# A hybrid decoder step on one core: gate logits from bfloat16 thirds over 99 contraction rows, with every engine's order found anew

## The chip, the core and the metric

One Trainium2 chip, one of its cores. A core has a matrix engine (TensorE, PE in the profile), a vector engine (VectorE, DVE), a scalar engine (ScalarE, ACT), a general engine (GpSimd, POOL) and an engine that here only issues DMAs (SyncE, SP). Each runs its own list of instructions in order; semaphores tie the lists together. PE's loads of weights (the stationary operand) are shown as PEld. The metric is the device time of one execution in microseconds; the kernel before was timed three times: 1186.76, 1187.25 and 1187.62 us, median 1187.25.

## The reference, cut to what matters

The reference is one layer of a decoder with two mixers side by side, for a prompt of 2048 tokens and for 8 samples of 8 tokens: dilated window attention, and gated linear attention (GLA) with 4 heads, key width 64 and value width 128. The change touches the gate of the second alone. The combined input projection gives, among others, 16 low-rank gate columns `g_lr` per token; from them come 4 x 64 gate logits:

```python
z = h @ w_in
q, k, v, qb, kb, vb, g_lr, gate_a, gate_b = jnp.split(z, split_points(), axis=-1)
log_a = jax.nn.log_sigmoid((g_lr @ w_gate_up + b_gate).astype(jnp.float32)) / GATE_TAU
o_b, s_fin = gla_chunked(heads(qb, H_B) * (DK_B ** -0.5), heads(kb, H_B), heads(vb, H_B),
                         heads(log_a, H_B), s0)
```

`g_lr` has 16 columns (GATE_RANK), `w_gate_up` is 16 x 256, `b_gate` has 256 entries, and everything is float32. The logs of the forget gates are summed over tokens, so the decay between any two tokens of a chunk hangs on them.

## The kernel before, in words

The program runs in stages that are woven together. The prompt is 16 tiles of 128 tokens. First come the projections for the window attention and that attention itself (matmuls `s`, transposes `t`, matmuls `O` at L1099 to L1132); then the projections `g`, `vb` and `gb` (matmuls at L1834, accumulators `acc_g`, `acc_vb`, `acc_gb`); last the output projection (`Y`, L2192) with the attention of the samples over their caches (`OS`, L2449). Large projections are split into two float16 parts and take three products. Dot products of cached keys (`pr` on POOL, L1689) fill the middle.

GLA runs beside `g`, `vb` and `gb`: one unit for the samples ("smp", 64 tokens), then eight units e0 to e7 of 256 prompt tokens (two chunks of 128). For each, `gla_core` (L838) loads the keys and queries (`zqk`) and the 16 gate columns (`zg`, L845) from device memory, where the projection has put them (L1452). It transposes `zqk` on PE (`ptg`, L870), and `zg` too: `pg` (L878), one PE transpose per 128 tokens in float32. ACT copies `pg` to `gT` (L879), a tile of 17 rows whose last row holds ones (a memset on POOL fills the tile first, L866). Two float32 matmuls with `wgu` (16 rows of `w_gate_up`, one row of `b_gate`) give the logits `u` for 256 tokens (L882). From there ACT and DVE make the log-sigmoid `la` (L888 to L891) and the decay `d` (L893). Then come seven levels: at each, PE makes scores `sc` and `sd` (L931), DVE selects them into `Ac` (L948), and `decay()` lets POOL scale keys (L907) and DVE scale queries (L911) and multiply the decays (L917) for the next level. After the levels PE makes the state update `U` (L1991) and the outputs `O` (L1999, L2005).

What runs beside it on POOL are `gw` (L1461), `Ac` (L855) and `prod` (L848); SP issues every DMA of the kernel, in one queue.

The order of all this is written out: after the program is traced, `in_order` (L747) chains each engine's instructions in the order of a long table of numbers, `ORDER`, one list for each of PE, DVE, ACT, POOL and SP. Where an instruction waits for a semaphore, all that stands behind it in its engine's list waits too.

## Time and profile before

| what | before |
|---|---|
| median of three runs | 1187.25 us (1186.76 to 1187.62) |
| profiled execution | 1188.94 us, of which the span from the first to the last instruction is 1187.2 |
| PE busy | 1158.4 us (98% of the span) |
| DVE / ACT / POOL busy | 909.4 / 739.2 / 547.0 us (77%, 62%, 46%) |
| chain that ended last | 89% PE, 7% DVE, 2% ACT |
| granted clock of PE | 0.998 of full, mean |

A row of the view of groups or of one line reads: line, engine, operation, output<-inputs, shapes, then busy time or durations. In a source view "374/374/478" is the least, median and greatest length in ns. A timeline row gives the start in us, the length in us, the engine and the operation; "x4" merges four records, and "[0.65 <-PE sd_e L931]" is the idle time ahead of it and who ended it. A row of waits gives who waited for whom: total us, times, longest. A row of windows gives, for a stretch of time, the busy time of PE, PEld, DVE, ACT and POOL with the number of instructions, then the clock, the share of DMA engines and GB/s. Matmuls are pipelined: their records overlap, so what one costs PE in a dense run is the time from its start to the next start.

### The profile page before, as it was taken

To read this page: it belongs to the slowest core of one execution; us is meant where nothing else is said; L and a number is where in the kernel's file an instruction comes from. 1 tells how busy PE (TensorE), PEld (TensorE's weight loads), DVE (VectorE), ACT (ScalarE), POOL (GpSimd) and SP (SyncE) were. 2 spreads that over 40 slices of the span, in tenths; PEclk is the share of its full clock that TensorE was granted. 3 is DMA by queue.
4 is the path that set the end of the run, shared out by engine and by line. 5 is a ranking of instruction groups with operands and counts; after the bars stand their busy time and mean duration, and the time that the engine had idled before them with its cause. 6 is when DMAs were issued, how large, how long until landed. Compare 5 with 4: busy or idle time off the path is not lost.

```text
span 1187.2 us, 28796 instructions
## 1 busy us (share of the span) xinstructions
PE 1158.4 (98%) x10386; PEld 713.4 (60%) x10386; DVE 909.4 (77%) x2540; ACT 739.2 (62%) x2042; POOL 547.0 (46%) x475
## 2 busy tenths in 40 slices
PE   5999999999999899999999999999999999999998
PEld 2544575566666666766777766646656656555543
DVE  7988788898888968778786755688988989734551
ACT  6655798788779967878777642654676654421220
POOL 0156444566548445662444567664545454311210
PEclk9999999999999999999999999999999999999999
DMA  8568967778976898899999878766773487999962
GB/s 295 192 196 215 254 170 167 187 230 256 216 199 179 205 250 286 271 255 277 273 267 269 249 255 233 220 195 200 253 241 114 139 283 253 332 400 403 379 201 80
DMA packets 235840, 283.24 MB, mean 239 GB/s; under 512 B 116193, under 2 KB 146866, under 8 KB 232626
## 3 DMA queue, kind: packets, MB, share of 16 engines
q1 hardware_dynamic: 235698, 281.40, 78.3%
q8 instruction: 82, 1.34, 0.5%
q14 instruction: 60, 0.49, 0.1%
HBM read 183.02 MB, written 75.24 MB: 218 GB/s over the span
## 4 chain that ended last, share of the span: by engine, by line
PE 89%; DVE 7%; ACT 2%; issue 1%; DMA 1%; POOL 0%; SPq 0%; DVEq 0%; POOLq 0%; ACTq 0%
PE Y L2192 12%; PE acc_g L1834 7%; PE acc_vb L1834 7%; PE acc_qkb L1834 7%; PE acc_k L1834 7%; PE acc_v L1834 7%; PE acc_q L1834 7%; PE acc_gb L1834 7%; PE t L1117 5%; PE s L1099 5%; PE O L1132 4%; PE OS L2449 2%; PE sc_e L931 2%; PE tm L2157 1%; PE O L2005 1%
## 5 line engine op out<-in xcount | busy, mean ns | idle before, releaser
L1689 POOL TENSOR_TENSOR pr<-k,qb 128x512 f32<-128x512 f32 x128 | 170.6, 1333 | 104.6 <-DVE sck L1690 86.2
L1834 PEld LDWEIGHTS <-hr 128*128 128x128 f16 x1824 | 165.1, 98 | 84.9 <-issue 3.5
L1132 PE MATMUL O<-v,pt 128*128 128x64 f16 x1800 | 211.6, 193 | 3.0 <-POOL pt L1084 1.9
L1110 ACT ACTIVATE p<-p,st 128x256 f32<-128x256 f32 (+1 forms) x384 | 173.3, 453 | 32.5 <-DVE st L1107 31.4
L2192 PE MATMUL Y<-w_o,mh 128*128 128x512 f16 x768 | 188.9, 379 | 0.1
L1132 PEld LDWEIGHTS <-pt 128*128 128x128 f16 x1800 | 146.0, 100 | 59.0 <-issue 3.7
L1834 PEld LDWEIGHTS <-hl 128*128 128x128 f16 x1248 | 117.4, 99 | 95.4 <-issue 3.3
L1084 POOL TENSOR_TENSOR pt<-p,pt 128x512 f16<-128x512 f32 (+1 forms) x80 | 95.2, 1190 | 164.9 <-ACT pt L1081 76.3
L1117 PE MATMUL t<-ident,p 128*128 128x128 f32 x600 | 149.6, 287 | 0.3 <-ACT p L1110 0.2
L1834 PE MATMUL acc_g<-w_g,hr 128*128 128x256 f16 (+1 forms) x768 | 131.6, 277 | 0.1
L1099 PE MATMUL s<-kk,qq 128*128 128x256 f16 (+1 forms) x512 | 115.3, 265 | 2.2 <-DVE st L1107 2.2
L1834 PE MATMUL acc_v<-w_v,hl 128*128 128x512 f16 x384 | 115.3, 385 | 1.1 <-ACT hl L1207 1.1
L1834 PE MATMUL acc_vb<-w_vb,hr 128*128 128x512 f16 x384 | 114.8, 379 | 0.0
L2192 PEld LDWEIGHTS <-mh 128*128 128x128 f16 x768 | 70.8, 98 | 68.0 <-issue 3.6
L1834 PE MATMUL acc_k<-w_k,hl 128*128 128x512 f16 x384 | 110.8, 379 | 0.0
L1834 PE MATMUL acc_q<-w_q,hl 128*128 128x512 f16 x384 | 110.5, 379 | 0.0
L1107 DVE CUSTOM_DVE_ANT_0 p<-s,m3w,scl_s 128x128 f32<-128x128 f32 (+1 forms) x256 | 92.8, 395 | 21.6 <-PE s L1099 12.5
L1690 DVE TENSOR_REDUCE sck<-pr 128x8 f32<-128x512 f32 x128 | 87.4, 682 | 24.7 <-POOL pr L1689 23.9
L1834 PE MATMUL acc_gb<-w_gb,hr 128*128 128x512 f16 x384 | 97.6, 380 | 0.0
L1117 PEld LDWEIGHTS t<-ident,p 128*128 128x128 f32 x600 | 80.9, 141 | 23.4 <-ACT p L1110 2.9
L1834 PE MATMUL acc_qkb<-w_qkb,hr 128*128 128x512 f16 x288 | 84.7, 379 | 0.0
L1110 ACT ACTIVATION_READ_ACCUMULATOR p<-p,st 128x1 f32 x384 | 73.2, 191 | 0.0
(545 smaller groups left out, 2461.4 us busy)
## 6 DMA issues: line engine op xcount, KB each, us to landing
k<-in_cache_k_win SPq DMA_DIRECT2D x104, 256.0 KB
sv_b<-in_cache_v_win SPq DMA_DIRECT2D x24, 1024.0 KB
hr<-h_d SPq DMA_DIRECT2D x44, 512.0 KB
qb<-q_d SPq DMA_DIRECT2D x64, 256.0 KB
oc<-o_d SPq DMA_DIRECT2D x48, 264.0 KB
o_d<-o SPq DMA_DIRECT2D x64, 132.0 KB
x<-in_x_prompt SPq DMA_DIRECT2D x16, 512.0 KB
h_d<-hl SPq DMA_DIRECT2D x16, 512.0 KB
```

Of the source, the lines that this page charges most:

```text
L931: PE.matmul(sc[j][k0 : k0 + 64, o : o + wide], k[js, t0 : t0 + 64], qv[js, t0 // (2 * B) : t0 // (2 * B) + max(1, 32 // B), 1, :], start=T ...
L1084: POOL.tensor_tensor(l, f, h, ALU.subtract)
L1099: PE.matmul(s_ps[:, i * w : (i + 1) * w], q, k, start=(n == 0), stop=(n == len(prods) - 1),)
L1107: DVE.tensor_tensor_reduce(s[:, sl], s_ps[:, sl], mask, neg, BIG, ALU.add, ALU.min, nmf(i))
L1110: ACT.activation(s[:, sl], s[:, sl], AF.Exp, bias=nmf(i), scale=-1.0, accum_out=denf(i))
L1117: PE.transpose(p_ps[:, i * P : (i + 1) * P], t["s"][:, i * P : (i + 1) * P], ident[:])
L1132: PE.matmul(o_, t["pt"][:, c, (i * nb + b) * P : (i * nb + b + 1) * P], vf(i, b)[:, d : d + HD], start=(b + n == 0), stop=(b == nb - 1 and ...
L1689: POOL.tensor_tensor(pr[:], kt, qt, ALU.mult)
L1690: DVE.tensor_reduce(out, pr[:].rearrange("p (u k d) -> p u k d", u=2, k=4), AX.X, ALU.add)
L1834: PE.matmul(z, a_[:, k, :], w[:, p_, k, cols], start=(k == 0 and i == 0), stop=(k == KT - 1 and i == 2),)
L2192: PE.matmul(Y[:], a_[:, k, :], w_[:, part, k, :512], start=(i == 0), stop=(i == len(prods) - 1),)
L2449: PE.matmul(OS[32 * x : 32 * x + 32, 0:256], ps(x), vs_[bb][:, 256 * u : 256 * u + 256], start=(i == 0), stop=(i == 13),)
```

## The change

Each gate column is written as a sum of three bfloat16 numbers (first, second, third), and so is each weight and bias. Six of the nine products of parts are kept (third x first, first x first, second x first, first x second, second x second, first x third), and instead of six matmuls the parts lie side by side along the contraction: 6 x 16 rows of features, and three rows of ones against the three parts of the bias, 99 rows. PE contracts them all in one bfloat16 matmul per 128 outputs.

- On POOL, per unit: a copy that narrows `zg` into three places of `gz` (`spread`, first parts), a subtraction for the rest `res`, a copy of `res` into two places (second parts), and a subtraction that writes the third parts. `gz` is one tile for all units, filled with ones once. The memset of `gT` is gone.
- On PE: `pg` transposes 99 bfloat16 columns of `gz` against a bfloat16 identity instead of 16 float32 columns of `zg`; `u` is a bfloat16 matmul.
- On ACT the copy `pg` to `gT` has 99 rows and stays bfloat16.
- Once, at the start of the stage: `wgf` is loaded (two DMAs, as `wgu` was), split into three parts by two ACT casts and two DVE subtractions, and six DMAs lay the parts out in `wgu` (99 x 256); a memset and a cast on POOL make `gz` and `identb`.
- The table `ORDER` is new for every engine.

Lines behind L862 stand 16 lines later in the changed file, those behind L1960 29 lines later: L931 is L947 there, L1999 is L2028.

```diff
--- before.py
+++ after.py
@@ -51,695 +51,695 @@
 ORDER = {
     "PE": (
-        "0 10 6 1-5 11 7 18 8 12 19-20 13 21 14 22 9 74 15 23 16 75 24 17 90 25 91 76 92 77 "
...
+        "0-7 10 18-19 11 20 12 21-22 13-16 74 23 17 8 24 9 25 75 90 76 91-99 77 100-103 78 "
...
@@ -835,6 +835,8 @@
         DVE.scalar_tensor_tensor(out, a[:n], 1.5, r[:n], ALU.add, ALU.mult)
 
 
+    GK = 99
+
     def gla_core(pools, st, row0, n, C, levels, mask, tagp, full=None):
 
         gl, gt, ps_t, ps_s, ps_p = pools
@@ -862,8 +864,22 @@
 
         kq = gt.tile([P, 2, 2, n], F32, name=f"kq_{tagp}", tag="kqg", bufs=3)
         kT, qT = kq[:, 0], kq[:, 1]
-        gT = gt.tile([17, n], F32, name=f"gT_{tagp}", tag="gT", bufs=2)
-        POOL.memset(gT[:], 1.0)
+        gz = st["gz"]
+        res = gt.tile([P, nch, 16], F32, name=f"res_{tagp}", tag="res")
+
+        def spread(first, count, x):
+            POOL.tensor_copy(
+                gz[:C, :nch, first : first + 33 * count].rearrange(
+                    "p c (s f) -> p c s f", f=33
+                )[:, :, :, :16],
+                x.unsqueeze(2).to_broadcast([C, nch, count, 16]),
+            )
+
+        spread(16, 3, zg[:C])
+        POOL.tensor_tensor(res[:C], zg[:C], gz[:C, :nch, 16:32], ALU.subtract)
+        spread(32, 2, res[:C])
+        POOL.tensor_tensor(gz[:C, :nch, 0:16], res[:C], gz[:C, :nch, 32:48], ALU.subtract)
+        gT = gt.tile([GK, n], BF16, name=f"gT_{tagp}", tag="gT", bufs=2)
         for c in range(nch):
             pt = ps_p.tile([P, 512], F32, name=f"ptg_{tagp}_{c}", tag="PT")
             for i in range(4):
@@ -873,14 +889,14 @@
             pv = pt[:, : 4 * C].rearrange("p (a c) -> p a c", a=4)
             ACT.activation(qT[:, :, c * C : (c + 1) * C], pv[:, 0:2, :], AF.Copy, scale=0.125)
             ACT.activation(kT[:, :, c * C : (c + 1) * C], pv[:, 2:4, :], AF.Copy)
-        pg = ps_p.tile([P, 512], F32, name=f"pg_{tagp}", tag="PT")
+        pg = ps_p.tile([P, 1024], BF16, name=f"pg_{tagp}", tag="PT")
         for c in range(nch):
-            PE.transpose(pg[:16, c * C : (c + 1) * C], zg[:C, c, :], ident[:C, :C])
-        ACT.activation(gT[:16, :], pg[:16, :n], AF.Copy)
+            PE.transpose(pg[:GK, c * C : (c + 1) * C], gz[:C, c, :GK], st["identb"][:C, :C])
+        ACT.activation(gT[:], pg[:GK, :n], AF.Copy)
         u = ps_p.tile([P, 512], F32, name=f"u_{tagp}", tag="PT")
         for p in range(2):
             PE.matmul(
-                u[:, p * n : (p + 1) * n], st["wgu"][:, p * P : (p + 1) * P], gT[:, :],
+                u[:, p * n : (p + 1) * n], st["wgu"][:, p * P : (p + 1) * P], gT[:],
                 start=True, stop=True,
             )
         la = gt.tile([P, 2, n], F32, name=f"la_{tagp}", tag="gt", bufs=2)
@@ -1948,16 +1964,29 @@
             SP.dma_start(
                 masks[r0 : r0 + 64], A["c_gmask"][r0 : r0 + 64, :, r0 // 2 : r0 // 2 + 32]
             )
-        wgu = gst.tile([17, 256], F32, name="wgu")
-        SP.dma_start(wgu[:16, :], A["w_gate_up"][0])
-        SP.dma_start(wgu[16:17, :], A["b_gate"])
+        wgf = gst.tile([17, 2, 256], F32, name="wgf")
+        SP.dma_start(wgf[:16, 0, :], A["w_gate_up"][0])
+        SP.dma_start(wgf[16:17, 0, :], A["b_gate"])
+        wgp = gst.tile([17, 3, 256], BF16, name="wgp")
+        ACT.activation(wgp[:, 0], wgf[:, 0], AF.Copy)
+        DVE.tensor_tensor(wgf[:, 1], wgf[:, 0], wgp[:, 0], ALU.subtract)
+        ACT.activation(wgp[:, 1], wgf[:, 1], AF.Copy)
+        DVE.tensor_tensor(wgp[:, 2], wgf[:, 1], wgp[:, 1], ALU.subtract)
+        wgu = gst.tile([GK, 256], BF16, name="wgu")
+        for part, r0, m in ((0, 0, 16), (0, 16, 16), (0, 32, 17), (1, 49, 16), (1, 65, 17),
+                            (2, 82, 17)):
+            SP.dma_start(wgu[r0 : r0 + m, :], wgp[:m, part])
+        gz = gst.tile([P, 2, GK + 17], BF16, name="gz")
+        POOL.memset(gz[:], 1.0)
+        identb = gst.tile([P, P], BF16, name="identb")
+        POOL.tensor_copy(identb[:], ident[:])
         Sbd = []
         ident64 = gst.tile([P, 64], F32, name="ident64")
         for r0 in (0, 64):
             DVE.tensor_scalar(
                 ident64[r0 : r0 + 64], ident[r0 : r0 + 64, r0 : r0 + 64], 0.125, None, ALU.mult
             )
-        st = {"wgu": wgu, "ident64": ident64}
+        st = {"wgu": wgu, "ident64": ident64, "gz": gz, "identb": identb}
         for i in range(2):
             t = gst.tile([P, 2, 256], F32, name=f"Sbd{i}")
             POOL.memset(t[:], 0.0)
```

The new lists differ from the old ones by short moves nearly everywhere; half of PE's matmuls stand at most 4 places from where they stood. Three places follow. The names carry the unit (e5, e6), the level of the scores and a buffer number at the end.

PE at the gate logits of unit e6 (`pg` and `u`), while the levels of e5 run; before:

```order
L878 MATMUL pg_e6_14484<-ident_79,zg_e6_14459 16x128
L1834 LDWEIGHTS hr_15_14366
L1834 MATMUL acc_gb_15_14612<-w_gb_12118,hr_15_14366 128x512
L878 MATMUL pg_e6_14484<-ident_79,zg_e6_14459 16x128
L2005 MATMUL O_8_13354<-vb_8_13347,full_10188 128x128
L1834 LDWEIGHTS hr_15_14366
L1834 MATMUL acc_gb_15_14612<-w_gb_12118,hr_15_14366 128x512
L1999 MATMUL O_8_13354<-Sbd0_10184,kq_e4_12900 128x256
L882 MATMUL u_e6_14488<-gT_e6_14468,wgu_10178 128x256 x2
L931 MATMUL sc_e5_16_13831<-kq_e5_13482 64x32 x2
```

and with the change:

```order
L1850 LDWEIGHTS hr_15_14410
L1850 MATMUL acc_gb_15_14660<-w_gb_12150,hr_15_14410 128x512
L2028 MATMUL O_8_13394<-Sbd0_10200,kq_e4_12936 128x256
L894 LDWEIGHTS gz_10193
L894 MATMUL pg_e6_14532<-identb_10195,gz_10193 99x128
L894 LDWEIGHTS gz_10193
L894 MATMUL pg_e6_14532<-identb_10195,gz_10193 99x128
L2034 MATMUL O_8_13394<-vb_8_13387,full_10204 128x128 x2
L2028 MATMUL O_8_13394<-Sbd0_10200,kq_e4_12936 128x256
L2034 MATMUL O_8_13394<-vb_8_13387,full_10204 128x128
L898 LDWEIGHTS wgu_10186
L898 MATMUL u_e6_14536<-gT_e6_14517,wgu_10186 128x256
```

`pg` now stands directly behind the first inter-chunk `O` and ahead of the other products; four `O` products and no `acc_gb` stand between it and `u`, and weight loads have rows of their own, since float32 matmuls load theirs within the instruction.

POOL at the same time, with the scaling of e5's keys (`kq_e5`, one row per level) and `gw`; before:

```order
L907 TENSOR_TENSOR kq_e4_12900<-kq_e4_12900,sums_e4_12932 128x4x64
L907 TENSOR_TENSOR kq_e5_13482<-kq_e5_13482,d_e5_13511 128x256
L907 TENSOR_TENSOR kq_e5_13482<-kq_e5_13482,sums_e5_13514 128x128x2
L907 TENSOR_TENSOR kq_e5_13482<-kq_e5_13482,sums_e5_13514 128x64x4
L1461 TENSOR_TENSOR gw_13_14518<-so_gb13_14511,gnw_395 128x512
L907 TENSOR_TENSOR kq_e5_13482<-kq_e5_13482,sums_e5_13514 128x32x8
```

and with the change:

```order
L923 TENSOR_TENSOR kq_e5_13522<-kq_e5_13522,d_e5_13555 128x256
L923 TENSOR_TENSOR kq_e5_13522<-kq_e5_13522,sums_e5_13558 128x128x2
L923 TENSOR_TENSOR kq_e5_13522<-kq_e5_13522,sums_e5_13558 128x64x4
L1477 TENSOR_TENSOR gw_13_14566<-so_gb13_14559,gnw_395 128x512
L881 TENSOR_TENSOR gz_10193<-res_e6_14512,gz_10193 128x2x16
L923 TENSOR_TENSOR kq_e5_13522<-kq_e5_13522,sums_e5_13558 128x32x8
L857 TENSOR_TENSOR Ac_e6_14509<-ident64_10197,dd_e6_14507 128x512
L871 CAST gz_10193<-zg_e7_15257 128x2x3x16
L879 TENSOR_TENSOR res_e7_15266<-zg_e7_15257,gz_10193 128x32
```

The last of e6's four operations (`gz<-res_e6,gz`) now stands between `gw_13` and the scaling for level 8, where nothing stood; e7's first copy follows two places later.

SP's queue where the sample's gate columns are loaded; before:

```order
L1952 DMA wgu_10178<-in_w_gate_up 16x256
L1701 DMA k3_6_2_7964<-in_cache_k_win 128x512
L1257 DMA hr_12_12136<-h_d_72 128x2048
L1457 DMA ga_d_65<-so_g19_12282 128x256
L1257 DMA hr_13_12363<-h_d_72 128x2048
L1953 DMA wgu_10178<-in_b_gate 1x256
L1699 DMA qb_6_2_7962<-q_d_58 128x512
L845 DMA zg_smp_10248<-zg_d_62 64x16
L843 DMA zqk_smp_10246<-zqk_d_61 64x512
L1704 DMA k2_6_3_8170<-in_cache_k_win 128x512
L1452 DMA zg_d_62<-zgs_9_12172 128x16
```

and, a little further down the queue with the change:

```order
L1715 DMA qb_6_6_8070<-q_d_58 128x512
L1717 DMA k3_6_6_8072<-in_cache_k_win 128x512
L847 DMA zg_e0_10619<-zg_d_62 128x2x16
L1470 DMA ga_d_65<-so_g010_12452 128x256
L845 DMA zqk_e0_10617<-zqk_d_61 128x2x512
L1468 DMA zg_d_62<-zgs_10_12449 128x16
L1978 DMA wgu_10186<-wgp_10181 16x256
L1978 DMA wgu_10186<-wgp_10181 17x256 x2
L1978 DMA wgu_10186<-wgp_10181 16x256
L1978 DMA wgu_10186<-wgp_10181 17x256
L1978 DMA wgu_10186<-wgp_10181 16x256
L1717 DMA k3_6_3_8168<-in_cache_k_win 128x512
```

The six copies into `wgu` stand ahead of the next load of cached keys, behind the loads of the first units; before, `wgu` was loaded from the inputs ahead of them.

1360 rows, old and new, of the table ORDER are left out of this document.

## The prediction

> **What bounds the kernel now.** I read the page first: engine shares, then the chain that ended last.
>
> ```profile
> span 1187.2 us, 28796 instructions
> PE 1158.4 (98%) x10386; PEld 713.4 (60%) x10386; DVE 909.4 (77%) x2540; ACT 739.2 (62%) x2042; POOL 547.0 (46%) x475
> PE 89%; DVE 7%; ACT 2%; issue 1%; DMA 1%; POOL 0%; SPq 0%; DVEq 0%; POOLq 0%; ACTq 0%
> ```
>
> PE covers 98% of the span and is 89% of the chain. Since a busy PE may still be a waiting PE (records overlap), I looked next at what PE waited for.
>
> ```profile
> PE mx_v L1269 <- DVE w_v L1326: 13.5, 1, 13.5
> PE s L1099 <- DVE st L1107: 2.2, 6, 0.6
> PE O L1132 <- POOL pt L1084: 1.9, 4, 0.6
> PE sc_e L931 <- DVE kq_e L911: 1.5, 1, 1.5
> ```
>
> All of PE's idle time is 1187.2 - 1158.4 = 28.8 us, and 13.5 us of it is one wait at the very start, which nothing here touches. So 15.3 us are left in the whole rest: PE is the bound, and PE time that goes away should come off the end nearly one for one. The changed lines run only between 700 and 950 us (the gated-linear-attention stage), so the chain of that stretch, cut into three windows (690 to 780, 780 to 870, 870 to 960 us), matters most:
>
> ```profile
> by line: PE acc_vb L1834 36.4%; PE acc_g L1834 35.7%; PE O_s L2058 4.1%; PE U_s L2091 3.8%; PE u_e L882 3.5%; PE ptg_e L870 3.4%; DVE kq_e L911 2.3%; PE acc_gb_s L1518 1.9%; PE acc_gb_s L1521 1.1%; PE sc_smp L931 1.1%; PE pg_e L878 0.9%; is
> by line: PE acc_gb L1834 53.3%; PE sc_e L931 12.8%; PE O L2005 6.4%; PE O L1999 5.2%; PE sd_e L931 4.3%; PE U L1991 3.7%; DVE kq_e L911 3.2%; PE u_e L882 3.0%; PE ptg_e L870 2.6%; PE U_s L2091 1.5%; PE ptk_e L973 1.1%; PE pg_e L878 0.8%; DV
> by line: PE acc_gb L1834 34.2%; PE sc_e L931 8.1%; PE O L1999 3.8%; DVE kq_e L911 3.5%; PE U L1991 3.2%; issue 3.1%; DVE Sbd L2012 3.0%; PE O L2005 3.0%; DVE Ac_e L948 2.6%; PE sd_e L931 2.2%; ACT mh L2158 2.0%; PE u_e L882 1.9%; DVE w_o L1
> ```
>
> The matmul that makes the gate logits, u (L882), is 3.5%, 3.0% and 1.9% of three 90 us windows: 3.2 + 2.7 + 1.7 = 7.6 us stand on the path that sets the end. Its transposes pg (L878) stand there too, with 0.9% and 0.8% in the first two.
>
> **The change, part by part.** Matmuls are pipelined, so I price them from start to the next start, not by their own length.
>
> ```profile
> 703.37 0.65 PE L882 MATMUL u_smp<-gT_smp,wgu 17*128 17x64 f32 x4
> 703.95 0.39 PE L1834 MATMUL acc_vb<-w_vb,hr 128*128 128x512 f16 x1
> ...
> 716.33 0.27 PE L878 MATMUL pg_e<-ident,zg_e 128*16 128x128 f32 x1
> 716.44 1.42 PE L1834 MATMUL acc_g<-w_g,hr 128*128 128x272 f16 x11
> 717.70 0.27 PE L870 MATMUL ptg_e<-ident,zqk_e 128*128 128x128 f32 x1
> ...
> 736.27 1.13 PE L882 MATMUL u_e<-gT_e,wgu 17*128 17x256 f32 x4
> 737.33 0.82 PE L1834 MATMUL acc_vb<-w_vb,hr 128*128 128x512 f16 x3
> ...
> 945.97 0.22 PE L2157 MATMUL tm<-ident,mt 128*128 128x128 f16 x1
> ...
> 947.76 0.67 PE L2157 MATMUL tm<-ident,mt 128*128 128x128 f16 x9
> ...
> L882 PE MATMUL u_e<-gT_e,wgu x32: 374/374/478, 736.3 to 945.4; 17*128 17x256 f32 x32
> L878 PE MATMUL pg_e<-ident,zg_e x16: 272/273/278, 716.3 to 943.5; 128*16 128x128 f32 x16
> ```
>
> *Removed: float32 u.* The program asks for two matmuls per chunk of 256 tokens, the trace holds 32 records for 8 chunks: each float32 matmul goes through PE twice. One chunk's four records take 737.33 - 736.27 = 1.06 us of PE. Eight chunks: 8.5 us; the sample's: 703.95 - 703.37 = 0.58 us.
>
> *Added: bfloat16 u.* No bfloat16 matmul is in the trace; the nearest row is the 2-byte acc_g with 272 columns, (717.70 - 716.44) / 11 = 0.115 us each. Two per chunk with 256 columns: 0.23 us at most, 1.8 us over eight, and under 0.1 for the sample. That 99 rows are contracted instead of 17 I price at nothing: 2-byte matmuls here contract 128 rows at 0.115. From below the cost cannot be under nothing, so u gains between 7.2 us and 9.1 us; I take 8.5 + 0.58 - 1.8 - 0.1 = **7.2 us**.
>
> *Transposes.* A float32 pg takes 716.44 - 716.33 = 0.11 us, a 2-byte one of the same 128 columns (0.67 - 0.22) / 8 = 0.056 us (0.22 is the length of a single tm, taken off a run of nine). 17 of them: **0.9 us** gained. Their weights grow from 16 to 99 columns; loads of weights run beside matmuls:
>
> ```profile
> L1834 PEld LDWEIGHTS <-hr 128*128 128x128 f16 x1824 | 165.1, 98 | 84.9 <-issue 3.5
> L1521 PEld LDWEIGHTS <-hs 128*64 128x64 f16 x64 | 2.9, 108 | 3.6 <-issue 2.1
> ```
>
> A 2-byte load is 98 to 108 ns. Hidden behind a 0.215 us neighbour (acc_vb: (0.82 - 0.39) / 2) it costs nothing; bare, behind a 0.056 us transpose, about 0.05. Bounds 0 and 17 x 0.05 = 0.9 us; I take 0.3, as most pg stand among long matmuls.
>
> *Added on POOL.* Per chunk: two copies that spread and narrow (96 and 64 elements a partition) and two subtractions (32), for one memset less.
>
> ```profile
> L2370 POOL COPY Scg<-Sc 128x256 f32<-128x256 f32 x4 | 1.6, 407 | 24.8 <-PE R L2375 12.9 <-DMA Sc<-sc_d 8.9 <-PE Y L2192 3.0
> L2043 POOL COPY qxs<-kq_smp 128x8 f32<-128x8 f32 x2 | 0.5, 241 | 0.1
> L907 POOL TENSOR_TENSOR kq_smp<-kq_smp,sums_smp 128x64 f32<-128x64 f32 x2 | 0.7, 360 | 2.1 <-PE sd_smp L931 1.8 <-POOL pr L1689 0.3
> L866 POOL MEMSET gT_e<- 17x256 f32 x8 | 2.4, 301 | 0.3 <-PE u_e L882 0.3
> ```
>
> Copies lie between 0.24 and 0.41, a small subtraction near 0.36: 4 x 0.35 = 1.4 us a chunk, 1.1 net of the memset, about 10 us over nine. POOL is 46% busy, so its own time is covered; if POOL were the bound it would cost these 10 us. What can reach PE is the order: the four run in line with the decays of the preceding chunk, and pg must wait for the fourth. For chunk e6 the new list puts the fourth right behind gw and ahead of the level-8 decay of e5. There POOL now has a hole:
>
> ```profile
> 915.87 1.27 POOL L1461 TENSOR_TENSOR gw<-so_gb,gnw 128x512 f32<-128x512 f32 x1
> 917.79 0.64 POOL L907 TENSOR_TENSOR kq_e<-kq_e,sums_e 128x256 f32<-128x256 f32 x1 [0.65 <-PE sd_e L931]
> ```
>
> 0.35 us fit into 0.65. The next chunk's first copy waits until PE has transposed this one (gz is one buffer), and that chunk's decays queue behind it; pg of e6 stands well ahead of that place in PE's list, so I price this wait at nothing, at most at one decay, 0.6 us a chunk.
>
> *POOL against DVE.* The decays of DVE show what POOL next to it does:
>
> ```profile
> L911 DVE TENSOR_TENSOR kq_e<-kq_e,sums_e x48: 375/420/1173, 784.7 to 1007.7; 128x256 f32<-128x256 f32 x48
> 900.00:930.00 30.00, 29.86 (x370) 19.50 (x369) 27.79 (x84) 23.36 (x54) 13.38 (x16) 1.00 0.34 112
> 930.00:960.00 30.00, 29.50 (x347) 17.54 (x347) 29.45 (x75) 17.56 (x39) 14.25 (x14) 1.00 0.58 184
> ```
>
> One form takes from 375 to 1173 ns: the longest exceeds the shortest by 0.8 us, more than a whole POOL decay (0.64 above). And DVE is full at 900 to 960 us (the columns are PE, PEld, DVE, ACT, POOL busy: 27.79 and 29.45 of 30 are DVE's). Two of the eight chunks (e6, e7) fall there, so POOL's added 2 x 1.4 = 2.8 us could become DVE's, and PE's. Bounds 0 and 2.8; I take 0.5, since PE still shows 29.5 and more busy there, with gb and Y matmuls to fill. [...]
>
> *Set-up.* The weights in thirds: two casts on ACT, two subtractions on DVE (17x256, each as the 0.30 memset to the 0.41 copy above: under 1 us beside PE), and eight DMAs on SP's queue for two.
>
> ```profile
> 687.88 0.43 SPq L1952 DMA_DIRECT2D wgu<-in_w_gate_up  x1
> 692.48 0.28 SPq L1953 DMA_DIRECT2D wgu<-in_b_gate  x1
> 695.22 0.49 SPq L845 DMA_DIRECT2D zg_smp<-zg_d  x1
> 702.36 0.22 PE L878 MATMUL pg_smp<-ident,zg_smp 64*16 64x64 f32 x1
> ```
>
> The six copies into wgu take 6 x 0.28 to 0.49 = 1.7 to 2.9 us of SP's queue, ahead of loads of cached keys. Landing: zg_smp, issued until 695.71, was there by 702.36, so under 6.7 us. In the new PE list 24 acc_g0, 15 acc_g1 and 24 acc_vb matmuls lie between tile 10's last acc_g1 and u_smp: 39 x 0.115 + 24 x 0.215 = 9.6 us (0.215 as above). About 1.5 us (scaling, a reduction, the subtraction on DVE) + 2.9 + 6.7 = 11.1 at worst, so 0 to 1.5 us of stall; I take 0, being nearer to the middle of the landing bound.
>
> *Sum.* 7.2 + 0.9 - 0.3 - 0.5 = **7.3 us**. The profiled execution took 1188.94 us (span 1187.2 and 1.7 around it), 1.7 above the median of 1187.25. 1188.9 - 7.3 = 1181.6, or on the runs' median 1187.25 - 7.3 = 1180.0.
>
> *The order.* All engines' lists were redone, but locally: half of PE's matmuls moved by at most 4 places, and no stage changed sides. What it can win is bounded by the 15.3 us of PE idleness, half of which I allow (7.6 us); what it can lose I bound by the same, 7.6. I take 0: nothing in the rows prefers a sign.
>
> **The rivals.**
> *The order eats it.* New handovers stall PE at other places (waits like the 2.2 and 1.9 us above grow). For it: thousands of places moved. Against it: the moves are short and PE has almost always filler. Losing 7.6 us gives 1187.6, no change.
> *DVE and POOL set the stage's end.* If the added POOL work blocks DVE in 900 to 960 fully and the weights come late: 7.3 + 0.5 - 2.8 - 1.5 = 3.5 us gain, 1183.7. For it: 29.45 of 30. Against it: PE is as full.
> *PE and POOL wait on each other* (the slow side). PE's list is strict; if pg stands at its head before POOL's fourth operation, everything behind stops, the scores too that POOL's next decay waits for. Price: one gw and a subtraction, 1.3 + 0.35 = 1.65 us a chunk, nine times 14.9 us, so 1187.25 - 7.3 + 14.9 = 1194.8. It decides from 7.3 / 9 = 0.8 us a chunk on. For it: gz's fourth operation and pg are close in the new lists at e6. Against it: the 0.65 us hole.
> *The order wins as well*: 1180.0 - 5 = 1175, if it closes a third of the 15.3 us.
>
> **How the numbers follow.** Forecast (1177 to 1183): 0.56. Order wins more: 0.08. DVE and POOL: 0.11. Order eats it: 0.15. PE and POOL wait: 0.10. A measurement tells 0.2%, 2.4 us, from no change, so faster means below 1184.9, slower above 1189.6. Faster: 0.56 + 0.08 + 0.09 = 0.73; same: 0.02 of the DVE case and 0.11 of the order's = 0.13; slower: 0.04 + 0.10 = 0.14. Predicted **1180 us**. The range, 1173.5 to 1188, holds the forecast, the order's gains and most of its losses, and leaves out the last rival.
>
> **What would show it.** Right: u with 16 records for the eight chunks at about 0.11 us to the next start; PE's busy time down by 7 to 9 us; its idle time near 28.8 us; u gone from the chain's shares. Wrong: PE idle ahead of pg or u released by POOL or ACT (PE and POOL wait); idle ahead of u_smp released by a DMA (late weights); DVE's L911 (L927 there) longer in the mean, with DVE in the chain at 900 to 960; or PE's idle time up by several us elsewhere, at lines that the change does not touch (the order).

## The result: 0.52% slower, and the profile after

The changed kernel took 1194.29 us in the median (1190.9 to 1195.07), the kernel before beside it 1187.25 us (1186.76 to 1189.05): a ratio of 1.0052, 95% interval 1.0035 to 1.007. The forecast was 1180 us. The profiled execution took 1194.29 us, with a span of 1192.5 us. From its page, the engine shares and the chain that ended last:

```profile
span 1192.5 us, 28754 instructions
PE 1154.2 (97%) x10368; PEld 710.1 (60%) x10368; DVE 910.5 (76%) x2542; ACT 738.5 (62%) x2044; POOL 560.9 (47%) x504
PE 77%; DVE 11%; ACT 3%; issue 3%; DMA 2%; POOL 1%; SPq 1%; DVEq 0%; POOLq 0%; ACTq 0%
```

PE is busy for 4.2 us less (1158.4 before), but it is idle for 1192.5 - 1154.2 = 38.3 us, where it was 28.8. So the time is not in what PE computes; PE stands still for 9.5 us more. The view of the gate's groups (line, engine, operation, output<-inputs, shapes, count, then busy us and mean ns of one, then the idle time ahead) shows that the edit does what it says:

```profile
L898 PE MATMUL u_e<-gT_e,wgu 99*128 99x256 bf16 x16 | 4.1, 275 | 0.0
L894 PE MATMUL pg_e<-identb,gz 128*99 128x128 bf16 x16 | 3.1, 222 | 0.0
```

One `u_e` and one `pg_e` in the timeline (start us, length us), each with the matmul that follows it:

```profile
722.10 0.22 PE L894 MATMUL pg_e<-identb,gz 128*99 128x128 bf16 x1
722.15 0.28 PE L886 MATMUL ptg_e<-ident,zqk_e 128*128 128x128 f32 x1
...
724.20 0.28 PE L898 MATMUL u_e<-gT_e,wgu 99*128 99x256 bf16 x1
724.31 0.28 PE L1850 MATMUL acc_g<-w_g,hr 128*128 128x272 f16 x1
```

16 records for eight chunks in place of 32, and 0.11 us from start to start. Summed over all units from start to next start, `u` went from 9.2 to 2.0 us and `pg` from 1.9 to 1.15 us: 8.0 us won on PE. What ate it shows first in the waits of PE (total us, times, longest):

```profile
PE mx_v L1285 <- DVE w_v L1342: 13.7, 1, 13.7
PE acc_vb L1850 <- DVE so_g L1385: 4.9, 1, 4.9
PE t L1133 <- ACT p L1126: 2.8, 2, 1.8
```

The first was there before (13.5 us). The other two are new (of the third, 0.2 us stood before), and both stand at lines that the change does not touch. In the chain of 690 to 780 us `u` has shrunk from 3.5% to 0.7%, and a DMA that was not in the list stands in it:

```profile
by line: PE acc_vb L1850 39.0%; PE acc_g L1850 36.2%; PE O_s L2087 4.1%; PE ptg_e L886 3.6%; PE U_s L2120 3.5%; DMA ga_d<-so_g 3.4%; PE acc_gb_s L1534 1.4%; PE sc_smp L947 1.1%; PE O_s L2094 0.8%; PE u_e L898 0.7%; PE O L1148 0.7%; SPq L172
```

To see where time is lost and won, the same PE instruction is looked up in two traces, and the difference of its start times is taken; the table gives the median of these differences over all matmuls that start within 15 us behind a mark of the profile before (us, plus is later than before). All kernels of the study are in it.

| kernel | 180 | 270 | 285 | 360 | 690 | 705 | 735 | 780 | 960 | 1110 | ratio to before, 95% interval |
|---|---|---|---|---|---|---|---|---|---|---|---|
| changed kernel | 0.3 | 1.1 | 3.1 | 4.7 | 4.3 | 10.3 | 9.3 | 5.4 | 4.1 | 4.8 | 1.0052 (1.0035 to 1.007) |
| e1 changed, old order | -0.6 | -0.6 | -0.6 | -0.6 | -1.8 | -2.4 | -3.4 | -4.2 | -3.8 | -3.8 | 1.0001 (0.999 to 1.0012) |
| e2 before, new order | -0.4 | 0.4 | 2.4 | 4.0 | 4.7 | 12.6 | 12.6 | 10.8 | 14.3 | 14.9 | 1.014 (1.0122 to 1.0158) |
| e3 changed, old order to 600 us | 0.0 | -0.1 | -0.1 | -0.1 | -0.9 | 3.7 | 2.7 | -1.2 | -3.4 | -2.9 | 0.9997 (0.9985 to 1.0008) |
| e4 changed, zg_smp moved | -0.1 | 1.5 | 3.5 | 5.1 | 3.5 | 3.5 | 2.4 | -1.5 | -3.7 | -3.2 | 0.9986 (0.9977 to 0.9996) |
| e5 e3 and e4 together | 0.0 | 0.0 | 0.0 | 0.0 | -0.4 | -0.5 | -1.5 | -5.4 | -7.6 | -7.1 | 0.9945 (0.9929 to 0.9961) |
| e6 before, order of e5 | 0.0 | 0.0 | 0.0 | 0.0 | -0.3 | 0.9 | 0.9 | -0.9 | 2.7 | 3.4 | 1.0032 (1.0021 to 1.0044) |
| e7 e5 without spreads | 0.3 | 0.2 | 0.2 | 0.2 | 0.1 | 0.0 | -1.0 | -4.9 | -5.2 | -4.7 | 0.9953 (0.9938 to 0.9969) |
| e8 e1 without spreads | -1.0 | -1.1 | -1.1 | -1.1 | -2.3 | -2.9 | -3.8 | -5.0 | -3.6 | -3.0 | 1.0001 (0.9989 to 1.0013) |
| e9 changed, rv_qk moved | 1.9 | 2.7 | 2.7 | 4.1 | 3.1 | 10.1 | 9.0 | 5.2 | 3.3 | 3.8 | 1.0038 (1.0024 to 1.0052) |
| e10 e4 and e9 together | 0.3 | 1.7 | 1.7 | 3.1 | 1.5 | 1.5 | 0.4 | -3.4 | -5.1 | -4.6 | 0.9971 (0.9961 to 0.9981) |
| e11 before, zg_smp early | -0.5 | -0.6 | -0.6 | -0.6 | -1.8 | 4.4 | 4.4 | 4.4 | 4.8 | 4.8 | 1.0045 (1.003 to 1.0059) |
| e12 changed, old order to 735 us | 0.6 | 0.6 | 0.6 | 0.6 | 0.9 | 0.3 | 6.7 | 3.1 | 0.8 | 1.3 | 1.0002 (0.9992 to 1.0012) |
| e13 e5, old order behind 960 us | -0.9 | -0.9 | -0.9 | -0.9 | -2.5 | -2.5 | -3.6 | -7.4 | -9.9 | -10.0 | 0.9934 (0.9922 to 0.9946) |
| e14 e5, old order behind 760 us | 0.3 | 0.3 | 0.3 | 0.3 | 0.1 | 0.1 | -1.0 | -4.5 | -3.0 | -3.0 | 0.9971 (0.9959 to 0.9982) |
| e15 changed, old order to 760 us | -1.2 | -1.2 | -1.2 | -1.2 | -2.4 | -3.0 | -4.0 | -3.2 | -5.0 | -4.5 | 0.9981 (0.997 to 0.9992) |

Rows with one and the same order up to 600 us (e1, e3, e5 to e8, e11 to e15) differ by up to 3.4 us at 690 us (-2.5 to 0.9), so a shift that runs through a row from early on is one execution's chance; what counts is a step inside a row, above all one that comes back in every row with the same order there. One such shift has a cause that can be seen: in the profile of the kernel before, PE waits 1.4 us at 547 us and is granted 0.91, 0.50 and 0.74 of its clock from 546 to 552 us. In e1 it waits as long there and keeps its full clock (1.00), so the 1.2 us that e1's row gains between 360 and 690 us are not the edit's. The changed kernel's row has four: a loss of some 4 us between 200 and 360 us, a loss of 6 us at 705 us, a win of 6 us from there to 960 us (the gate), and a loss of about 1 us behind 960 us.

Two theories stood against each other. *The order*: the two losses are the new order's, and the gate's gain is there. *The program*: POOL's new instructions, the one `gz` buffer and the set-up of `wgu` cost what was lost. In the experiments' traces line numbers are off by one to three, as their tables of the order have other lengths.

### The profile page after: what moved, and what is told of

Same layout as the page of the kernel before. It is cut to its first block, busy times and chain, and to the rows that moved or that the text cites. A ratio compares the mean times of both kernels' runs of the same rounds, so it can differ in the third digit from the quotient of the medians.

```text
span 1192.5 us, 28754 instructions
## 1 busy us (share of the span) xinstructions
PE 1154.2 (97%) x10368; PEld 710.1 (60%) x10368; DVE 910.5 (76%) x2542; ACT 738.5 (62%) x2044; POOL 560.9 (47%) x504
## 4 chain that ended last, share of the span: by engine, by line
PE 77%; DVE 11%; ACT 3%; issue 3%; DMA 2%; POOL 1%; SPq 1%; DVEq 0%; POOLq 0%; ACTq 0%
PE Y L2221 11%; PE acc_vb L1850 7%; PE acc_g L1850 7%; PE acc_qkb L1850 6%; PE acc_k L1850 6%; PE acc_q L1850 5%; PE t L1133 5%; PE acc_gb L1850 5%; PE acc_v L1850 5%; PE s L1115 5%; PE O L1148 4%; PE OS L2478 2%; PE sc_e L947 2%; PE tm L2186 1%; DVE p L1123 1%
## 5 line engine op out<-in xcount | busy, mean ns | idle before, releaser
L1148 PE MATMUL O<-v,pt 128*128 128x64 f16 x1800 | 216.8, 193 | 1.4 <-ACT pt L1092 0.6
L1850 PE MATMUL acc_g<-w_g,hr 128*128 128x272 f16 (+1 forms) x768 | 130.9, 276 | 0.0
L1123 DVE CUSTOM_DVE_ANT_0 p<-s,m3w,scl_s 128x128 f32<-128x128 f32 (+1 forms) x256 | 92.3, 395 | 16.6 <-PE s L1115 5.7
L2263 POOL TENSOR_TENSOR oc<-oc 128x512 f32<-128x512 f32 x32 | 40.2, 1270 | 78.9 <-DVE oc L2256 48.2
```

Source lines behind the costliest of these rows:

```text
L1123: DVE.tensor_tensor_reduce(s[:, sl], s_ps[:, sl], mask, neg, BIG, ALU.add, ALU.min, nmf(i))
L1148: PE.matmul(o_, t["pt"][:, c, (i * nb + b) * P : (i * nb + b + 1) * P], vf(i, b)[:, d : d + HD], start=(b + n == 0), stop=(b == nb - 1 and ...
L1850: PE.matmul(z, a_[:, k, :], w[:, p_, k, cols], start=(k == 0 and i == 0), stop=(k == KT - 1 and i == 2),)
L2263: eng.tensor_tensor(o_[g], o_[g], w[:, g].unsqueeze(2).to_broadcast([P, NH, HD]), ALU.mult)
```

## The experiments

**e1 and e2: program and order exchanged.** e1 is the changed program in the order before. Nearly every row of the table `ORDER` differs; the core is where the set-up stands on SP (651 and 652 are the `wgf` loads, 653 to 658 the `wgu` transfers, 663 the load of `zg_smp`, 662 that of `zqk_smp`):

```diff
-        "645 513 739 741 512 649 743 652 646 518 517 744 742 663 496 524 745 525 523 750 754 662 "
+        "723 494 644 734 736 735 638 732 501 448 503 641 502 507 737 642 506 651-652 514 740-741 "
+        "513 742 739 512 738 645 518 646 525 745 496 517 524 743 656 655 657 750 754 523 653 658 "
```

> The changed program (thirds of features and weights, one gz buffer, the wgu set-up, all 38 new GpSimd instructions) with the order of the kernel before on every engine; only the new instructions are put in: the two wgf loads at 675 us of the profile before, the four casts and subtractions at 684 to 688 us, the six wgu transfers at 689 to 695 us, a unit's four GpSimd instructions after its zg has landed. Theory 'the order': the local gain of 7.3 us is there and nothing is lost elsewhere, 1187.3 - 7.3 = 1180 us (1178 to 1183). Theory 'the program': the GpSimd instructions, the one gz buffer and the set-up cost what was lost, whatever the order, 1190 us or more (never under 1187).

> The program before (float32 u and pg, no spreads) with the order of the changed kernel on every engine; the memsets of gT stand where the first spread of a unit stands, the two wgu loads where the wgf loads stand. Theory 'the order': without the gain of the gate and with the loss of the new order, 4 to 5 us in the attention stage and some 6 us round 700 us, 1187.3 + 10 = 1197 us (1193 to 1200). Theory 'the program': 1187 us (1185 to 1190).

e1: 1188.97 us, ratio 1.0001. e2: 1205.33 us, ratio 1.014. Neither theory was right about both. The new order costs the program before 1.4%, some 16.6 us of 1187.5, more than the 10 expected, so the order is at fault; but the order before does not bring the changed program its gain either. e1 was not the end of the case: where had its 7.3 us gone? First the losses.

**e3: the order before up to 600 us.** The table's rows are those of the kernel before for all that starts there before 600 us.

```diff
-        "0-7 10 18-19 11 20 12 21-22 13-16 74 23 17 8 24 9 25 75 90 76 91-99 77 100-103 78 "
+        "0 10 6 1-5 11 7 18 8 12 19-20 13 21 14 22 9 74 15 23 16 75 24 17 90 25 91 76 92 77 "
...
```

> The changed program; every engine goes by the order before for what starts there before 600 us of the profile, and by the new order for the rest. Theory 'the order', first part: the 4.5 us that PE falls behind between 200 and 330 us of the span are given back, 1194.3 - 4.5 = 1190 us (1188 to 1191.5). Theory 'the program' (all its new work lies behind 600 us): no difference, 1194 us (1192.5 to 1195.5).

1187.16 us, ratio 0.9997. The loss between 200 and 360 us is gone from the row, and 0.55% from the time, 6.5 us where 4.5 were expected (below the range stated). What the theory of the program says (no difference) falls: none of the new work lies ahead of 600 us.

**e9: the half of that loss that has one cause.** At 287 us the changed kernel shows one odd row. DVE's `rv_qk`, a scaling of 16 numbers a partition, in the timeline of the kernel before, with the two POOL products beside it:

```profile
286.20 0.17 DVE L829 TENSOR_SCALAR rv_qk<-qs_q 128x16 f32<-128x16 f32 x1
285.00 1.27 POOL L1425 TENSOR_TENSOR t_qk<-zs_q,ct_qk 128x512 f32<-128x512 f32 x1
286.23 2.37 POOL L1419 TENSOR_TENSOR t_qk<-zs_q,ct_qk 128x1024 f32<-128x1024 f32 x1
```

and in that of the changed kernel:

```profile
287.30 2.40 DVE L829 TENSOR_SCALAR rv_qk<-qs_q 128x16 f32<-128x16 f32 x1
286.08 1.28 POOL L1441 TENSOR_TENSOR t_qk<-zs_q,ct_qk 128x512 f32<-128x512 f32 x1
287.31 2.36 POOL L1435 TENSOR_TENSOR t_qk<-zs_q,ct_qk 128x1024 f32<-128x1024 f32 x1
```

Before, it starts 0.03 us ahead of the second product and is through after 0.17 us. In the changed kernel it starts 0.01 us ahead of it and ends at 287.30 + 2.40 = 289.70, just behind that product's end (287.31 + 2.36 = 289.67). DVE's next instructions, ACT's `p` and PE's transposes `t` stand behind it (the 1.8 us wait above). That the product held `rv_qk` up is the author's reading of the two ends, 0.03 us apart; by what means, no trace shows. The experiment moves `rv_qk` (563) ahead of one copy (510) on DVE, so that it comes while the first product runs:

```diff
-        "505-506 498 520 508 441 509 521-522 501 507 511 451 549 562 531-532 534 510 563 535 530 "
+        "505-506 498 520 508 441 509 521-522 501 507 511 451 549 562 531-532 534 563 510 535 530 "
```

> The changed kernel with one DVE instruction moved by one place: rv_qk of token tile 11 (0.17 us when nothing holds it, 2.40 us at 287.3 us of the profile, where it ends with GpSimd's t_qk) goes ahead of the copy of an O tile, so that it comes while the GpSimd product before is still running and gets in between the two. Theory 'a collision of DVE with GpSimd': it takes 0.2 to 0.5 us, PE's wait for the p of the attention (1.8 us) goes, 1194.3 - 2 = 1192.3 us, and PE's delay against the kernel before falls by 2 us behind 290 us. Rival 'ACT or DVE is late there anyway': the 1.8 us stay, 1194 us.

1192.92 us, ratio 1.0038 (0.14% below the changed kernel; the intervals overlap, so the times alone would not settle it). In the trace:

```profile
288.56 0.42 DVE L829 TENSOR_SCALAR rv_qk<-qs_q 128x16 f32<-128x16 f32 x1
287.69 1.26 POOL L1441 TENSOR_TENSOR t_qk<-zs_q,ct_qk 128x512 f32<-128x512 f32 x1
288.91 2.37 POOL L1435 TENSOR_TENSOR t_qk<-zs_q,ct_qk 128x1024 f32<-128x1024 f32 x1
```

It takes 0.42 us and again ends 0.03 us behind a product, this time the first (288.98 against 288.95). PE's wait of 1.8 us is gone, and the step of 2 us between 270 and 285 us is missing in its row. The rest of the front's loss, some 3 us in small steps, was not taken apart further.

**e4: one load on SP's queue.** In the changed kernel SP's timeline has a hole (a row is one DMA that SP issues; the write of `so_g` into `ga_d` is what DVE must wait for before it refills that buffer):

```profile
688.59 0.43 SPq L1489 DMA_DIRECT2D vb_d<-vbs  x1
698.88 0.50 SPq L847 DMA_DIRECT2D zg_smp<-zg_d  x1
...
700.59 0.38 SPq L1470 DMA_DIRECT2D ga_d<-so_g  x1
...
702.06 0.38 SPq L1473 DMA_DIRECT2D ga_d<-so_g  x1
```

The view of waits names the cause:

```profile
SPq L847 <- PE O L1148: 9.2, 1, 9.2
```

and the timeline shows who paid: DVE waits for the `ga_d` write, PE for DVE.

```profile
703.71 0.48 DVE L1385 TENSOR_SCALAR so_g<-acc_g,wi_g 128x256 f32<-128x256 f32 x1 [7.44 <-DMA ga_d<-so_g]
...
704.25 2.29 PE L1850 MATMUL acc_vb<-w_vb,hr 128*128 128x512 f16 x5 [4.89 <-DVE so_g L1385]
```

`zg_smp` is put into memory that the last matmuls `O` of the attention still read. Its load waits for them, as it did before (2.4 us there), but in the new list both writes of `so_g` stand behind it, whereas in the kernel before they stood ahead:

```profile
685.88 0.32 SPq L1454 DMA_DIRECT2D ga_d<-so_g  x1
...
691.26 0.33 SPq L1457 DMA_DIRECT2D ga_d<-so_g  x1
...
695.22 0.49 SPq L845 DMA_DIRECT2D zg_smp<-zg_d  x1
```

The experiment moves this one instruction (663) to just ahead of the load of `zqk_smp` (662):

```diff
-        "645 513 739 741 512 649 743 652 646 518 517 744 742 663 496 524 745 525 523 750 754 662 "
+        "645 513 739 741 512 649 743 652 646 518 517 744 742 496 524 745 525 523 750 754 663 662 "
```

> The changed kernel with one instruction moved: on SP's queue the load of zg_smp stands eight transfers later, right ahead of the load of zqk_smp, so that the writes of so_g09 and so_g19 into ga_d no longer stand behind its wait of 9.2 us. Theory 'the order', second part: the stall of 4.9 us on PE at 704 us and part of what follows go, 1194.3 - 6 = 1188 us (1186 to 1190). Theory 'the program', or the wait only passes to the next transfer: 1194 us (1192 to 1195.5).

1186.76 us, ratio 0.9986. SP's wait is down to 2.7 us, PE waits for nobody between 690 and 730 us, and the step at 705 us is gone (3.5 and 3.5), which the rows of e2, e3 and e9, with `zg_smp` at its new place, all have. The six `wgu` transfers keep their places in the list, so they cost PE nothing that this trace shows.

**e11: the same wait put into the kernel before.** The load of `zg_smp` (657 there) moves ahead of the write of `so_g09` (739):

```diff
-        "733 512 732 645 518 646 525 739 496 517 651 524 737 744 748 652 523 657 656 544 738 536 "
+        "733 512 732 645 518 646 525 657 739 496 517 651 524 737 744 748 652 523 656 544 738 536 "
```

> The kernel before with one instruction moved: the load of zg_smp, eleven places forward on SP's queue, to stand ahead of the write of so_g09 into ga_d, as in the changed kernel. Theory 'the queue': the load waits for the last O matmuls of the attention with the two ga_d writes behind it, PE stands 4 to 5 us for so_g and is then granted a lower clock for some us, 1187.5 + 6 = 1193.5 us (1191 to 1196). Rival 'only the changed kernel's set-up (six wgu transfers, two wgf loads) makes the stall': 1187.5 us (1186 to 1189).

1193.71 us, ratio 1.0045, and a step of 6.2 us at 705 us. The place of one load in a queue makes the whole step, with none of the change's instructions in the program. Its waits show both links:

```profile
SPq L845 <- PE O L1132: 10.0, 1, 10.0
...
PE acc_vb L1834 <- DVE so_g L1369: 2.6, 1, 2.6
PE acc_g L1834 <- DVE so_g L1369: 1.4, 1, 1.4
```

The waits sum to 4.0 us, the step to 6.2. Most of the rest goes with a lower clock. In the windows of e11 behind the longer wait (the columns are PE, PEld, DVE, ACT and POOL busy, then PE's granted clock), PE's busy time times the share of the clock that is missing gives an estimate of its cost, 1.35 x 0.31 + 2.0 x 0.50 = 1.4 us:

```profile
696.00:698.00 2.00, 1.35 (x5) 0.70 (x5) 0.48 (x1) 1.31 (x3) 0.00 (x0) 0.69 0.48 157
698.00:700.00 2.00, 2.00 (x7) 0.84 (x6) 0.00 (x0) 0.03 (x1) 0.66 (x1) 0.50 0.88 213
```

In those of the changed kernel:

```profile
702.00:704.00 2.00, 0.00 (x0) 0.00 (x0) 0.29 (x1) 0.00 (x0) 0.00 (x0) 1.00 0.73 248
704.00:706.00 2.00, 1.75 (x5) 0.65 (x5) 1.44 (x4) 1.65 (x4) 0.00 (x0) 0.53 0.56 164
706.00:708.00 2.00, 2.00 (x9) 0.95 (x8) 0.43 (x3) 0.00 (x0) 0.00 (x0) 0.61 0.98 362
708.00:710.00 2.00, 2.00 (x15) 1.20 (x14) 0.98 (x2) 0.57 (x2) 1.80 (x3) 1.00 1.03 269
```

After the stall PE is granted 0.53 and 0.61 of its clock for some 3.75 us of work, by the same estimate 1.75 x 0.47 + 2.0 x 0.39 = 1.6 us on top of the 4.9. The matmuls show it: the five `acc_vb` from 704.25 us on take (706.33 - 704.25) / 5 = 0.42 us each from start to start, and at 734 us, with the clock at 1.00, three take 0.65 us, 0.22 each. Lower clocks also followed shorter waits: 2.6 us in e11 (0.69 and 0.50 above), 2.5 us in e12 (0.50) and 1.4 us in e5 (0.90, 0.50 and 0.74, below). Behind e11's other wait of 1.4 us the clock stayed at 1.00. What sets it, no trace shows.

**e5, e10 and e6: the repairs together.** e5 has e3's front and e4's load, e10 has the changed kernel's order with only the two moved instructions of e4 and e9, and e6 is the program before in the order of e5 (its memsets of `gT` where a unit's first spread stands).

> The changed program with both repairs of the order together: the order before for what starts there before 600 us, the new order for the rest, and the load of zg_smp moved on SP's queue to stand right ahead of zqk_smp's. Theory 'the order': the two losses lie at different places and add up (4.5 us in the attention stage, 4.8 to 6 us at 704 us), 1187.2 - 4.8 = 1182.4 us from the one repair and 1186.8 - 4.5 = 1182.3 us from the other, so 1182 us (1180 to 1184.5). Rival 'something behind takes it back' (DVE, over 0.9 busy from 810 to 960 us, sets the end of the stage whichever time it is entered): 1185 to 1187 us.

> The changed kernel with that one DVE instruction and the load of zg_smp moved, two instructions in all. Theory 'two places': 1186.8 - 2 = 1184.8 us (1183.5 to 1186.5). Rival: no better than the load alone, 1186.8 us.

> The program before (float32 u, no spreads) in that same repaired order: what the edit itself is worth where the order is the same on both sides. Theory 'the order': the 7.3 us of the sum, so 1182 + 7.3 = 1189.5 us (1187 to 1192). If the new order and not the edit brings the time down: 1182 to 1184 us.

e5: 1181.67 us, ratio 0.9945; e10: 1184.74 us, ratio 0.9971; e6: 1192.31 us, ratio 1.0032. The losses lie at separate places and add up. Two instructions moved turn a kernel 0.52% slower into one 0.29% faster. And with the same order on both sides the edit is worth 1.0032 - 0.9945 = 0.87%, 10.3 us; between e2 and the changed kernel, again with one order, 0.88%. That is 2 us more than the 8.0 us of its own rows; the trace of e6 accounts for about one of them (its `u` takes 10.2 us from start to start, not 9.2), and the other is open.

**e7 and e8: the price of POOL's new work.** In e5 and in e1 the four POOL instructions a unit are left out, so that the logits come from constant features:

```diff
-        spread(16, 3, zg[:C])
-        POOL.tensor_tensor(res[:C], zg[:C], gz[:C, :nch, 16:32], ALU.subtract)
-        spread(32, 2, res[:C])
-        POOL.tensor_tensor(gz[:C, :nch, 0:16], res[:C], gz[:C, :nch, 32:48], ALU.subtract)
```

> The repaired changed kernel without the four GpSimd instructions of each unit (two spreads, two subtractions; gz keeps its ones, so the gate logits are those of constant features): the price of the 1.1 to 1.2 us of GpSimd a unit and of their wait ahead of pg. Theory 'GpSimd is covered': within 1 us of the kernel with them, 1181 to 1183 us. Rival 'GpSimd delays the gate or DVE': 2 us or more below it, under 1180.5 us.

> The changed program in the order before (1188.5 us, no gain seen) without the same four GpSimd instructions a unit. If GpSimd ate the gain there: 1181 to 1184 us. If PE, which now comes to DVE's results too early in an order that was laid out for the slower gate, waits for DVE instead: no difference, 1187 to 1189 us.

e7: 1183.03 us, ratio 0.9953, against 0.9945 with them. e8: 1188.86 us, ratio 1.0001, as with them. POOL's work is covered in both orders, to within the intervals (some 0.15% to both sides); the theory of the program is out, and POOL is not what keeps e1's gain away.

**e12, e14 and e15: where the order lets the gain through.** e12 and e15 are the changed program in the order before up to 735 and 760 us and in the repaired new order behind; e14 is e5 up to 760 us and the order before behind. The edits are again rows of the table.

> The changed program in the order before up to 735 us of the profile before (with the set-up, the samples' unit and SP's queue of that order), the new order only behind it. Where the order decides whether the edit's gain arrives: if in the stage of the prompts' chunks (735 to 960 us), where DVE is over 0.9 busy, 1182 us as with the new order from 600 us on (1180 to 1184); if already round 700 us, 1186 to 1188.5 us as with the order before throughout.

> The repaired changed kernel with the order before for what starts behind 760 us. Its PE is 3 to 3.5 us ahead of the kernel before at 760 us and 7.6 us at 960 us. Theory 'in the stage of the prompts' chunks only the new order turns PE's shorter gate into time, the old one into waits for DVE': what was won by 760 us stays and nothing is added, 1187.9 - 3.5 = 1184.4 us (1183 to 1186). Rival 'the order round 700 us decides, and not that stage': 1181.7 us (1180.5 to 1183).

> The other way round: the changed program with the order before up to 760 us and the new order behind. Theory of that stage: 2.4 us won by 760 us as with the order before throughout, and 3.7 us behind it, 1187.9 - 6.1 = 1181.8 us (1180.5 to 1184), if no new stall stands at the seam. Rival: 1187 to 1188.5 us.

e12: 1188.06 us, ratio 1.0002, and it tells nothing. At its seam PE has nothing left but one chain (`u`, the log-sigmoid, the next transposes) and waits 2.5 us for DVE's `la`, with the clock at 0.50 behind it, a step of 6.4 us at 735 us; from there to 960 us it then wins 5.9 us. e14: 1184.31 us, ratio 0.9971, as expected: the 3.5 us of lead at 765 us stay (3.0 at the end), where e5 went on to 7.6. e15: 1184.56 us, ratio 0.9981, 3 us above what was expected; it has a seam too (from 4.8 us ahead at 750 us to 1.7 at 765 us, with PE idle for 1.9 of the 5 us from 755 us on), but behind it the lead grows by the 3.7 us of the forecast, from 1.7 to 5.4 us at 990 us. So between 760 and 960 us only the new order turns a shorter gate into time. The table says the same for 735 to 960 us, with the program before as well. With the edit in the new order PE wins 5.2 to 6.3 us there (e7, without POOL's work, 4.2); without the edit in the new order it loses 1.7 and 1.8 us (e2, e6); with the edit in the order before it wins 0.4 (e1) or loses 0.2 (e8). So a part of the 0.87% is what the new order costs the slower gate. What becomes of it in the order before shows in one window (columns as above), in this order of the kernel before, of e1, of e14 and of e5:

```profile
760.00:960.00 200.00, 197.87 (x2358) 118.03 (x2356) 178.53 (x494) 126.90 (x295) 101.82 (x102) 1.00 0.59 195
```

```profile
760.00:960.00 200.00, 194.20 (x2350) 115.41 (x2347) 181.75 (x498) 125.22 (x292) 106.07 (x117) 1.00 0.59 194
```

```profile
760.00:960.00 200.00, 194.45 (x2351) 115.70 (x2350) 180.21 (x497) 124.93 (x291) 106.72 (x116) 1.00 0.61 200
```

```profile
760.00:960.00 200.00, 196.69 (x2388) 118.32 (x2385) 183.82 (x507) 127.61 (x297) 111.25 (x118) 1.00 0.61 207
```

PE is idle for 2.1 us before, for 5.8 and 5.6 us with the edit in the old order (e1, e14), for 3.3 us with the edit in the new one (e5), where DVE does more in the same 200 us (183.8 us). PE's waits in 690 to 960 us of e1, which the kernel before has only in part (1.5 us for `kq_e`, 0.4 for `full`), name DVE:

```profile
PE sc_e L947 <- DVE kq_e L927: 1.7, 2, 1.5
PE sc_e L947 <- DVE Ac_e L964: 1.6, 2, 0.9
PE ptg_e L886 <- DVE la_e L907: 0.8, 2, 0.6
PE mx_gb L1285 <- DVE la_e L907: 0.6, 1, 0.6
```

One thing about e1 stays open. Its executions took 1185.16 to 1190.62 us, and the profiled one, with 1185.44, is among the three shortest: in it PE ends 3.8 us ahead, where the median shows no gain. The five with a granted clock of 0.996 or 0.997 took 1188.43 us and more; what lowers the clock in them, no trace shows.

**e13: the last stage.** e5 with the order before for what starts behind 960 us.

> The repaired changed kernel (order before up to 600 us, new order with zg_smp moved behind it) with the order before again for what starts behind 960 us. Theory 'the new order costs a little in the last stage too' (PE's delay of the changed kernel grows from 3.8 us at 990 us to 5.3 us at the end): 1181.7 - 1.5 = 1180.2 us (1179 to 1181.5). Rival 'that growth is one profile's': 1181.7 us (1181 to 1183.5).

1179.32 us (1178.96 to 1181.21), ratio 0.9934, 95% interval 0.9922 to 0.9946: the new order does seem to cost something behind 960 us too. The interval overlaps with e5's, so the times alone do not settle it; the rows speak for it. All eleven rows with the new order there lose 0.5 to 0.7 us from 960 to 1110 us, and of the five with the order before only e8 does. Behind that, at 1150 us, e5's trace has a wait that e13's has not, with granted clocks of 0.90, 0.50 and 0.74 from 1150 to 1156 us:

```profile
PE mt_s L2199 <- DVE mix_s L2293: 1.4, 1, 1.4
```

This is the best kernel of the study, 0.66% below the one before. Its page:

```profile
span 1177.2 us, 28799 instructions
PE 1146.8 (97%) x10368; PEld 708.3 (60%) x10368; DVE 911.3 (77%) x2542; ACT 738.8 (63%) x2044; POOL 559.9 (48%) x504
```

PE's idle time is 30.4 us, near the 28.8 before, and none of the two new waits is left.

## Why the prediction was wrong, step by step

- *PE is the bound; what is taken from PE comes off the end nearly one for one.* Right for the new order, where e5 and e13 have the gain in the time. In the order before it holds only for a part: PE was 197.87 of 200 us busy from 760 to 960 us, and yet most of its shorter work there became waits for DVE (e1, e14). A PE that is nearly always busy was read as slack everywhere else; DVE's 178.5 of 200 us says how little there was.
- *u 7.2 us and transposes 0.9 us.* Right: 9.2 to 2.0 us and 1.9 to 1.15 us from start to start, 8.0 us where 8.1 were forecast. A bfloat16 `u` takes 0.113 us, as the row of `acc_g` said.
- *Loads of weights 0.3 us.* A load for `pg` takes 126 ns (that of 128 columns 98), and `pg` shows 56 ns to the next start nonetheless. Too small to be seen.
- *POOL's four instructions covered, 0; POOL against DVE 0.5 us, up to 2.8.* The four take 3.9 + 2.7 + 2.6 + 2.4 = 11.6 us over eight units, 1.45 us a unit, as forecast (266 + 338 + 236 + 254 = 1094 ns in the medians; a few are much longer). e7 and e8 price both at nothing that can be measured. L927 is hardly longer (502 ns in the mean of 48, 491 before), and its other form is shorter (432 ns in the mean of eight, 882 before). One DVE instruction did last as long as the POOL product beside it (`rv_qk`, 2.40 us against 2.36), but it is one that the change does not touch, 400 us earlier.
- *Set-up 0, at most 1.5 us.* Right: e4 keeps it as it is, and PE waits for nobody there between 690 and 730 us.
- *The order 0, bounds 7.6 us to both sides.* This is the step that failed. e13 against the changed kernel says what the order's bad places cost: 1.0052 - 0.9934 = 1.18%, 14.0 us: 7.8 for the place of `zg_smp` (e4), 1.8 for `rv_qk` (e10 against e4), 3.1 for the rest of the front (e5 against e10) and 1.3 behind 960 us (e13 against e5). The parts of 1.8 and 1.3 us (0.15% and 0.11%) are about as small as the intervals are wide, so their sizes are not sure. With 7.8 us to be won, 6.2 were lost. Two arguments behind the step were wrong. PE's idle time bounds what an order can win; it says nothing of what it can lose, since a new wait needs no old idleness. And "half of PE's matmuls moved by at most 4 places" was counted on PE, while the costly move was one DMA of SP, past two writes that DVE waits for. The text had the row of that load (695.22 us) and the rule (all that stands behind a waiting instruction waits too, as SP's 9.2 us show), but did not ask what the new list puts behind it.
- *The rivals.* "PE and POOL wait on each other" gave 1194.8 us, by luck 0.5 us from the result, and was wrong in all its steps: without POOL's instructions nothing changes (e7, e8). "The order eats it" was the right mechanism, too small by its bound (1187.6 us). "DVE and POOL set the stage's end" was half right, in the order before: DVE without POOL.
- *What would show it.* Of the signs, "PE's idle time up by several us elsewhere, at lines that the change does not touch" came true, and it led to the cause. Of the signs for right, `u` has its 16 records of 0.11 us, but PE's busy time fell by 4.2 us and not by 7 to 9: it mixes the edit with the order. Between programs in one order it fell by 8.4 us (1158.4 before, 1150.0 in e1) and by 8.6 (1160.5 in e6, 1151.9 in e5).

## What to carry to other kernels

When every engine's list changes, look in each in-order queue for the instructions that wait long, and compare what stands behind them before and after: a DMA that waited for memory to come free held everything queued behind it (for 9.2 us in the changed kernel, 10.0 us in e11), and the place of one load cost here nearly what the whole edit saves (0.66% against 0.87%). Bound the loss by the waits that a new list can make, not by the idle time of the old one. And price an edit in one and the same order on both sides: here it was worth 0.87% in a new one and, by the medians, nothing in the old. An edit's worth hangs on the order it is priced in.

## What was not expected of the hardware

- A DVE instruction took 0.17 us where it started 0.03 us ahead of a GpSimd product, and 2.40 us where it started 0.01 us ahead of it; there it ended 0.03 us after that product. One place earlier it took 0.42 us.
- A stall of 4.9 us on PE was followed by granted clocks of 0.53 and 0.61 over 4 us, by estimate 1.6 us more to pay; e11 shows 0.69 and 0.50 behind a stall of about 2.6 us, and e12 0.50 behind one of 2.5 us. Behind one and the same wait of 1.4 us at 547 us the clock fell to 0.50 in the profile before and stayed at 1.00 in e1's.
- The six small transfers into `wgu` held SP for 542 to 666 ns each (586 in the median), against 428 and 283 ns for the two loads into `wgu` before.
